# A 64 KB-strided transfer of sixteen half rows in front of all loads of a rotation kernel

## The chip, the cores and the metric

The kernel runs on one core of a Trainium2 chip. The metric is the device time of one execution in microseconds (us). A core has a matrix engine (TensorE, not used here), VectorE, ScalarE and GpSimd for computing, SyncE for issuing transfers, and 16 DMA engines that carry the transfers between the device memory (HBM) and the core's memory (SBUF, 128 partitions).

## The reference

A batch of 32 x 3 pictures of 256 x 256 float32 values is rotated by 90 degrees; nothing is calculated on the values.

```python
x = np.random.randn(32, 3, 256, 256).astype(np.float32)

def reference(x):
    return np.rot90(x, k=-1, axes=(-2, -1)).astype(np.float32)
```

That is 25.17 MB in and 25.17 MB out. Output row i of a picture is input column i read from the bottom up, so each picture is transposed and mirrored.

## The kernel before

**Tiling.** All 24,576 input rows (32 x 3 x 256, 1 KB each) are held in SBUF at once, in four groups of 2, 2, 4 and 4 units; a unit is 2048 rows, 16 KB in each of the 128 partitions. Each group has a tile of its own (`u0` to `u3`, printed as `u` in the profile), so no buffer is used for a second load. Three scratch tiles stand beside them: `spare` (two halves in PSUM), `extra` and `most`.

**Loads.** SyncE issues all of them, in the order in which they are written, on one hardware queue. Group 0 comes first and in two transfers: L67 brings the first 1024 rows (1 MB, eight consecutive rows or 8 KB to each partition, into the last quarter of the tile), L68 the other 3 MB. Partition p of the first transfer takes rows 8p to 8p + 7, so eight neighbouring partitions hold 64 KB of consecutive input. Group 1 follows in two transfers of 2 MB (L79), groups 2 and 3 in two of 4 MB each (L42, the helper `wide`). That makes eight loads. None of them waits for anything.

**Compute.** VectorE turns 32 x 32 blocks (`turn`, L92), ScalarE copies (`copy`, L95). The helper `keep` ties each instruction of an engine to the one before it, so both engines run in the order in which the calls are written. VectorE's first transpose needs both transfers of group 0.

**Stores.** Eight, again issued by SyncE in order, behind all loads: group 0 first (L200, made to wait for a mark in ScalarE's order, and one through `wide`), then two each for groups 1 to 3 (L42). Each waits for VectorE and ScalarE to be done with its half of a group.

**Semaphores.** The framework gives every transfer one of eight DMA semaphores in turn. With eight loads and eight stores each semaphore serves one load and one store. At the end SyncE (L236) waits until all of them have reached their counts.

The lines that the change touches are the two loads of group 0:

```python
    ld = rows_of(rows_in, 0).rearrange("(b p r) w -> p b (r w)", b=4, p=P)
    home = groups[0].rearrange("p s f -> p (s f)").rearrange("p (b f) -> p b f", b=4)
    nc.sync.dma_start(out=home[:, 3], in_=ld[:, 0])
    nc.sync.dma_start(out=home[:, :3], in_=ld[:, 1:])
```

Of the kernel before, what the change touches and what calls it, by code (L numbers as in the profile page):

```python
# [9 lines left out]
def kernel(  # L10
# [14 lines left out]
    nc = tc.nc  # L25
    fp32 = mybir.dt.float32

    B, C, H, W = x.shape
    P = nc.NUM_PARTITIONS
    R = 16  # L30
# [30 lines left out]
    def rows_of(rows, n):  # L61
        return rows[first[n] * P * R : (first[n] + sizes[n]) * P * R]


    ld = rows_of(rows_in, 0).rearrange("(b p r) w -> p b (r w)", b=4, p=P)
    home = groups[0].rearrange("p s f -> p (s f)").rearrange("p (b f) -> p b f", b=4)
    nc.sync.dma_start(out=home[:, 3], in_=ld[:, 0])  # L67
    nc.sync.dma_start(out=home[:, :3], in_=ld[:, 1:])  # L68
    for n in range(1, len(sizes)):
        I = sizes[n]  # L70
        ld = rows_of(rows_in, n).rearrange("(a i m r) w -> i m a (r w)", a=2, i=I, m=P // I)
        to = groups[n].rearrange("p s f -> p (s f)").rearrange("p (a f) -> p a f", a=2)
        if I == 4:
            ld = rows_of(rows_in, n).rearrange("(a i m r) w -> a m i (r w)", a=2, i=I, m=P // I)
# [166 lines left out]
```

## Time and profile before

| | |
|---|---|
| median of 3 runs | 122.49 us (122.31 to 122.51) |
| profiled execution | 122.36 us |
| its span, from the first to the last instruction | 120.6 us |
| moved over HBM | 50.33 MB, 417 GB/s over the span |
| DMA queue, share of 16 engines | 97.4% |
| VectorE busy | 83.3 us (69%), 25 instructions |
| ScalarE busy | 41.9 us (35%), 22 instructions |
| first load (L67), issue to landing | 4.8 us, 1 MB |
| VectorE's first transpose starts | 13.09 us |

Times inside the execution are counted from the start of the span. A row of the page such as `DMA` or `GB/s` has 40 numbers, one for each fortieth of the span (3.0 us); a digit is a share in tenths. Queue rows give packets, megabytes, and the time that the packets took as a share of 16 engines' span. A row of the waits says who waited for whom: microseconds in total, times, the longest. `SPq` is SyncE's instruction queue, and `L` with a number is a line of the kernel; L236 is the end of the program. A row of the chain or of the timeline begins with the start and the length in microseconds. Besides these views the trace holds a record of each DMA packet (start, length, size) and of each semaphore's updates, from which a few numbers below are taken.

### The profile page before, as it was taken

The page shows a single profiled execution, that of the slowest core. Times are in us where ns is not written, and L with a number is a line of the kernel's source. Part 1 is how long each engine was busy: PE and PEld are TensorE (multiplying, and loading weights), DVE is VectorE, ACT ScalarE, POOL GpSimd, SP SyncE. Part 2 cuts the span into 40 slices and gives each one's busy share as a digit, 9 for nine tenths or more (in the row PEclk, how much of TensorE's full clock was granted, in tenths as well). Part 3 has the DMA queues.
Part 4 walks back from the last instruction along what each step waited for, and adds up shares of the span by engine and source line. Part 5 has one row for each costly group of instructions (what it writes and reads, how often), then busy time and mean ns, then how long its engine had stood idle before and what let it go on. Part 6 is the DMA issues. An engine that isn't in the chain of part 4 may idle for free.

```text
span 120.6 us, 124 instructions
## 1 busy us (share of the span) xinstructions
DVE 83.3 (69%) x25; ACT 41.9 (35%) x22; POOL 0.2 (0%) x4
## 2 busy tenths in 40 slices
DVE  0000699999999999999999999999999900000000
ACT  0000400006910099937859389808302900000000
POOL 0000000000000000000000000000000000000000
DMA  3999999998989899999989999999898989898983
GB/s 95 429 427 427 454 429 435 435 500 370 489 380 489 380 435 435 413 457 402 467 370 500 391 478 391 478 391 478 380 489 380 489 380 489 370 500 359 511 359 163
DMA packets 2368, 50.33 MB, mean 417 GB/s; under 512 B 256, under 2 KB 256, under 8 KB 256
## 3 DMA queue, kind: packets, MB, share of 16 engines
q1 hardware_dynamic: 2368, 50.33, 97.4%
HBM read 25.17 MB, written 25.17 MB: 417 GB/s over the span
## 4 chain that ended last, share of the span: by engine, by line
DVE 68%; DMA 10%; issue 2%; SPq 0%; DVEq 0%
DVE u L92 48%; DVE spare L92 13%; DMA u<-in_x_dram 10%; DVE extra L92 5%; DVE most L92 2%; SPq L67 0%; DVEq L92 0%
## 5 line engine op out<-in xcount | busy, mean ns | idle before, releaser
L92 DVE STREAM_TRANSPOSE u<-u 128x2048 f32<-128x2048 f32 x15 | 56.0, 3792 | 0.2
L92 DVE STREAM_TRANSPOSE spare<-u 128x2048 f32<-128x2048 f32 (+1 forms) x4 | 11.7, 2946 | 13.1 <-DMA u<-in_x_dram 13.1
L95 ACT COPY u<-spare 128x2048 f32<-128x2048 f32 (+2 forms) x9 | 13.2, 1518 | 6.7 <-DVE spare L92 3.8
L95 ACT COPY spare<-u 128x2048 f32<-128x2048 f32 x2 | 7.6, 3811 | 8.9 <-DMA u<-in_x_dram 8.8
L95 ACT COPY extra<-u 128x1024 f32<-128x1024 f32 (+1 forms) x3 | 6.4, 2122 | 2.0 <-DMA u<-in_x_dram 2.0
L95 ACT COPY u<-extra 128x1024 f32<-128x1024 f32 (+2 forms) x4 | 6.0, 1670 | 2.7 <-DVE extra L92 2.7
L95 ACT COPY u<-u 128x2048 f32<-128x2048 f32 x1 | 1.9, 1899 | 13.7 <-DVE u L92 13.7
L95 ACT COPY u<-most 128x1792 f32<-128x1792 f32 x1 | 3.3, 3287 | 7.3 <-DVE u L92 7.3
L95 ACT ACT_TABLE_LOAD x1 | 1.3, 1283 | 13.1 <-DMA u<-in_x_dram 13.1
L92 DVE STREAM_TRANSPOSE spare<-spare 128x2048 f32<-128x2048 f32 x2 | 4.6, 2308 | 0.0
L92 DVE STREAM_TRANSPOSE u<-extra 128x2048 f32<-128x2048 f32 x1 | 4.0, 4004 | 0.0
L92 DVE STREAM_TRANSPOSE extra<-u 128x2048 f32<-128x2048 f32 x1 | 3.9, 3895 | 0.0
L95 ACT COPY most<-u 128x1792 f32<-128x1792 f32 x1 | 3.2, 3217 | 0.0
L92 DVE STREAM_TRANSPOSE extra<-extra 128x2048 f32<-128x2048 f32 x1 | 2.3, 2312 | 0.0
L92 DVE STREAM_TRANSPOSE most<-most 128x1792 f32<-128x1792 f32 x1 | 2.0, 1991 | 0.0
L225 POOL MEMSET const-bfloat16-1.0<- 128x1 bf16 x1 | 0.1, 102 | 0.0
L225 POOL MEMSET const-uint8-127<- 128x1 uint8 x1 | 0.1, 102 | 0.0
L225 POOL MEMSET const-float32-0.0<- 128x1 f32 x1 | 0.1, 100 | 0.2 <-issue 0.2
L225 POOL MEMSET const-float32-1.0<- 128x1 f32 x1 | 0.1, 99 | 0.0
## 6 DMA issues: line engine op xcount, KB each, us to landing
u<-in_x_dram SPq DMA_DIRECT2D x4, 4096.0 KB, 43.0
out_dram<-u SPq DMA_DIRECT2D x4, 4096.0 KB, 19.3
out_dram<-u SPq DMA_DIRECT2D x4, 2048.0 KB, 14.7
u<-in_x_dram SPq DMA_DIRECT2D x2, 2048.0 KB, 18.3
u<-in_x_dram SPq DMA_DIRECT2D x1, 3072.0 KB, 11.8
u<-in_x_dram SPq DMA_DIRECT2D x1, 1024.0 KB, 4.8
```

The source lines that it names most:

```text
L92: keep(nc.vector.transpose(out=out, in_=in_))
L95: keep(nc.scalar.copy(out=out, in_=in_))
L225: nc = _bacc.Bacc("TRN2", target_bir_lowering=False, num_devices=1)
```

## The change

A strip of 16 partitions with 128 float32 values each (512 bytes a partition) is allocated behind all other SBUF tiles. In front of the two loads of group 0, SyncE issues a transfer into it: of the partitions' rows in the first load's view every eighth (`ld[::P // R, 0]`, with P = 128 and R = 16), and of each the first 128 values. So it reads 16 pieces of 512 bytes whose starts are 64 KB apart; these are the first half of input rows 0, 64, 128 and so on up to 960. The first load reads the same bytes again into its own place. Nothing reads the strip.

```diff
     ld = rows_of(rows_in, 0).rearrange("(b p r) w -> p b (r w)", b=4, p=P)
     home = groups[0].rearrange("p s f -> p (s f)").rearrange("p (b f) -> p b f", b=4)
+
+    strip = ctx.enter_context(tc.tile_pool(name="strip", bufs=1)).tile([R, W // 2], fp32, name="strip")
+    nc.sync.dma_start(out=strip, in_=ld[::P // R, 0, : W // 2])
     nc.sync.dma_start(out=home[:, 3], in_=ld[:, 0])
     nc.sync.dma_start(out=home[:, :3], in_=ld[:, 1:])
     for n in range(1, len(sizes)):
```

## The prediction

> **What bounds the kernel now.** I read the page's DMA rows first, because the kernel moves 50.33 MB and computes nothing but transposes.
>
> ```profile
> DMA  3999999998989899999989999999898989898983
> GB/s 95 429 427 427 454 429 435 435 500 370 489 380 489 380 435 435 413 457 402 467 370 500 391 478 391 478 391 478 380 489 380 489 380 489 370 500 359 511 359 163
> q1 hardware_dynamic: 2368, 50.33, 97.4%
> ```
>
> The 16 DMA engines are busy from the second slice to the last but one: one queue, issued by SyncE alone, holds them 97.4% of the span. Only the first slice (3 tenths) and the last are open. So the end is fixed by the moment the engines begin to stream, plus 50.33 MB at their pace, as long as the queue never runs dry. The next views ask whether it does.
>
> ```profile
> SPq L42 <- DVE u L92: 27.8, 2, 20.2
> SPq L236 <- DMA out_dram<-u: 20.9, 3, 9.7
> 57.99 0.66 SPq L200 DMA_DIRECT2D out_dram<-u  x1
> 58.69 39.96 SPq L42 DMA_DIRECT2D out_dram<-u  x7
> ```
>
> The first two lines are SyncE's waits, the last two its issues in the timeline. SyncE issues the last store at 97.40, then waits 20.9 us at the end for DMAs (L236). By the semaphore records the last load lands at 61.63, when the first store (57.99) has been in the queue for 3 us. The last two stores, issued at 96.76 and 97.40, have 3 us in hand before the store ahead of them lands at 100.40. The queue never empties, so VectorE's chain, which the page shows as 68% of the span, is covered; it ends at 96.69.
>
> The change sits at the other end, so the chain of waits up to the first transpose comes next:
>
> ```profile
> 0.67 0.06 issue
> 0.73 0.40 SPq L67
> 1.12 0.06 issue
> 1.18 11.80 DMA u<-in_x_dram
> 12.98 0.03 issue
> ```
>
> And the same stretch in windows of 0.25 us. The columns at the end are the granted clock, the engines' busy share (a packet counted where it starts) and GB/s:
>
> ```profile
> 1.50:1.75 0.25, 0.00 (x0) 0.00 (x0) 0.00 (x0) 1.00 0.00 0
> 1.75:2.00 0.25, 0.00 (x0) 0.00 (x0) 0.00 (x0) 1.00 1.42 262
> 2.00:2.25 0.25, 0.00 (x0) 0.00 (x0) 0.00 (x0) 1.00 0.37 66
> 2.25:2.50 0.25, 0.00 (x0) 0.00 (x0) 0.00 (x0) 1.00 0.20 66
> 2.50:2.75 0.25, 0.00 (x0) 0.00 (x0) 0.00 (x0) 1.00 0.78 295
> 2.75:3.00 0.25, 0.00 (x0) 0.00 (x0) 0.00 (x0) 1.00 1.03 426
> ```
>
> Full pace is 426 GB/s, reached at 2.75. The packet records say how it gets there. A first batch of eight engines starts its first 8 KB packet at 1.77 to 1.96; the second batch of eight starts at 2.54 to 2.69, 0.77 us behind. In the first batch a first or second packet takes 0.46 to 1.06 us where the steady packet takes 0.309, and all of these long ones but one end between 2.78 and 2.90. Nothing like it occurs later. Each engine has a fixed share of the rows, so **the last engine to start sets the end**. It starts at 2.688, its second packet at 3.051; with the steady step of 0.306 per packet its virtual start is 3.051 - 0.306 = 2.745. The 16 landings of the first load are spread over 0.49 us, those of the last store over 0.54: the start's spread is carried through to the end.
>
> **The change part by part.**
>
> *One more issue on SyncE.* The strip's copy is issued first and L67 behind it. The nearest row is L67's own 0.397 us (128 rows, one dimension); L68 takes 0.419, and the loads of two dimensions 0.62 to 0.72. The strip has 16 rows in one dimension, so I take 0.397, with 0.72 as the upper end. The lower end is nothing: no row shows what an issue of 16 rows costs. With the gap of 0.058 to the next issue (1.125 to 1.183) the first load is issued 0.455 us later. Every later load moves by as much on SyncE's queue, and costs nothing there, because the transfers queue behind the first. L67's issue has no cover: SyncE's barrier ends at 0.67 and no other engine is moving data.
>
> *16 packets of 512 B and their 16 semaphore writes.* The load is landed by 16 engines; I take one row of the strip to each, at the address where that engine's share of the first load begins (its eight rows of 8 KB are 64 KB). Bounds: the 4-byte packet takes 0.009 us, the 8 KB packet 0.309. By size a row is 512/8192 x 0.309 = 0.02 us, with its semaphore 0.03 us. Engines that are idle until the load's descriptors come hide it; without that cover it is 0.03 us.
>
> *One more user of the eight DMA semaphores.* There are eight loads and eight stores for eight semaphores; with the strip the eighth load shares the strip's, and may wait for it before its issue. That issue comes at 5.11 + 0.455 = 5.57. The first load, 128 times as large, lands at 5.54, and the strip stands ahead of it, so I take nothing; if that issue did wait, it has until about 52 us, when its turn in the queue comes. The stores move by one semaphore together with the loads. At the end SyncE waits for the same eight.
>
> *What is behind it.* VectorE's first transpose waits for L67 and L68, so it shifts with the loads; so do all stores. The 3 us in hand at 61.63 and at 100.40 stay as they are, since both sides shift alike. Nothing else on VectorE, ScalarE or GpSimd is touched, and the strip's 512 bytes per partition are allocated behind all other tiles.
>
> *What the strip does to the start of the load behind it.* This is the one unknown. After the change the last engine may begin the load as late against its own issue as now: +0.455. Or the slow start belongs to the first use of the queue and is spent on the strip. If it were wholly gone and all engines started the load as far behind its issue as the very first does now (1.04 us), the last would start at 1.183 + 1.04 = 2.22, which is 2.22 - 2.745 = -0.52. So the ends are -0.52 and, with the dearest issue, 0.72 + 0.06 = +0.78. I take the first reading, +0.455. The eight late engines are late as a batch of half the 128 rows, and their packets are not stretched (0.31 to 0.38): they look as if they wait for the first batch's rows to be set up, as each new issue must have it done, rather than for a memory that is still asleep.
>
> The Trainium skill, page "DMA: Bandwidth & Descriptors", section "Latency and other measured facts", gives about 600 ns to the first byte of a DMA issued from SyncE. The trace agrees for the first batch, 1.77 - 1.125 = 0.64 us behind the end of the issue, and not for the second, 1.41 us. If that figure held for all engines once the queue is in use, an estimate from that page would have the load start by 1.58 + 0.6 = 2.18 and the run some 0.5 us faster, as the second rival below has it from rows alone; no transfer in this trace starts in an empty queue but the first, so the trace cannot decide.
>
> *Sum.* 122.36 (profiled execution: span 120.58 and 1.78 around it) + 0.455 = 122.81. The median of the runs, 122.49, is 0.13 above that execution, and so the forecast is 122.49 + 0.455 = **122.94**, slower by 0.37%.
>
> **The rivals.**
>
> *The slow start is paid once, at a fixed time (no change that can be told).* The strip's row waits where the load's first packet waits now. For it: the long packets end together at 2.78 to 2.90 although they started up to 0.58 us apart, as at one event. Then the late batch gets its strip row at 2.54 to 2.69 and the load 0.03 later: +0.03. Engines of the first batch that hold their strip until 2.89 start the load there with nothing read yet, at 2.89 against 2.745: +0.15. Result 122.52 to 122.64. Against it: four of the first eight packets took only 0.35 to 0.45, so there was no general standstill.
>
> *The strip wakes the path (faster).* The start-up is short for 16 packets of 512 B, and the load finds all engines ready: first start 2.22, the last one up to 0.19 later (the first batch's own spread), 2.41. Against 2.745 that is -0.52 to -0.33: 121.97 to 122.16, centre 122.1. It decides as soon as the last engine starts the load before 2.745 - 0.245 = 2.50. For it: the second batch waits about as long as eight rows on each of eight engines may take to set up (64 rows in 0.77 us, 12 ns each), and the strip has one row each, 0.1 us. Against it: by the same reckoning the load's own second batch would wait again, and nothing shows that a second set-up is quicker.
>
> On this rival the Trainium skill, same page, section "Two DMAs through the same engine are not ordered", says that descriptors of one queue start in order but are pipelined, so the load need not wait for the strip's write. No run here shows that yet; it would leave the forecast alone and take weight from the next rival.
>
> *The lag twice, or a dearer issue (slower by more).* The issue costs 0.62 to 0.72 as the two-dimensional loads do, or the load's set-up starts only when the strip is through at 2.89: +0.65 to +0.9, about 123.2.
>
> **How the numbers follow.** Differences under 0.2% (0.245 us) I count as no change: the three runs of before span 122.31 to 122.51. Forecast (+0.3 to +0.6): 0.49. Wake-up (faster): 0.25. Paid once (same): 0.20. Twice or dearer: 0.06. Slower is 0.49 + 0.06 = 0.55. The range starts at 122.05, inside the wake-up's 121.97 to 122.16 so that most of it is held, and ends at 123.10, the forecast's +0.6; that leaves out some 0.10 below and 0.07 above. The forecast's own range is 122.79 to 123.10. Cases of both signs hold most of the chance, so the range is one of 0.9% about a start-up of 1 us.
>
> **What would show it.** Right: in the changed profile SyncE's queue has one more issue of about 0.4 us ahead of the load's at about 1.18; the rise to 426 GB/s comes at about 3.2 instead of 2.75; the first load lands at about 6.0 instead of 5.54, the first transpose starts at about 13.54 instead of 13.09; and the end moves by as much. Full pace by 2.4 would show the wake-up, by 2.8 that the start-up is paid once. The prediction is wrong if the second batch is late only in the queue's first transfer. If the first transpose starts later and the end does not move, or the reverse, then the reading that the queue never runs dry was wrong.

## The result and the profile after

| | before | after |
|---|---|---|
| median | 122.40 us (6 runs, 122.31 to 122.51) | 122.92 us (6 runs, 122.87 to 122.99) |
| profiled execution's span | 120.6 us | 121.1 us |
| first load issued | 0.73 | 1.18 |
| first load landed (last engine) | 5.53 | 6.02 |
| first transpose starts | 13.09 | 13.58 |
| last load landed | 61.63 | 62.12 |
| last store landed | 119.76 | 120.23 |

The changed kernel takes 1.0042 times as long, with a 95% interval of 1.0029 to 1.0055. The forecast was 122.94, slower by 0.455 us; measured is 0.52 between the medians and 0.47 between the last landings of the two traces. That 122.94 and 122.92 lie so close is partly luck: the kernel before came out at 122.40 here, 0.09 under the 122.49 that the forecast starts from, and the change is 0.065 larger than its 0.455.

The chain of waits up to the first transpose, answering the one of before:

```profile
0.73 0.39 SPq L69
1.12 0.06 issue
1.18 0.41 SPq L70
1.58 0.04 issue
1.62 11.86 DMA u<-in_x_dram
13.48 0.03 issue
```

L69 is the strip's issue, L70 the first load's (L67 before), L71 the second's. Ahead of the DMA stand now two issues of about 0.4 us, and the DMA's own stretch is as long as it was: from L71's issue 11.86, before 11.80.

The windows at the start (granted clock, the engines' busy share, GB/s at the end of a row; a packet is counted where it starts):

```profile
1.75:2.00 0.25, 0.00 (x0) 0.00 (x0) 0.00 (x0) 1.00 0.13 31
2.00:2.25 0.25, 0.00 (x0) 0.00 (x0) 0.00 (x0) 1.00 0.56 131
2.25:2.50 0.25, 0.00 (x0) 0.00 (x0) 0.00 (x0) 1.00 0.72 131
2.50:2.75 0.25, 0.00 (x0) 0.00 (x0) 0.00 (x0) 1.00 0.89 131
2.75:3.00 0.25, 0.00 (x0) 0.00 (x0) 0.00 (x0) 1.00 0.59 164
3.00:3.25 0.25, 0.00 (x0) 0.00 (x0) 0.00 (x0) 1.00 0.52 164
3.25:3.50 0.25, 0.00 (x0) 0.00 (x0) 0.00 (x0) 1.00 0.87 360
3.50:3.75 0.25, 0.00 (x0) 0.00 (x0) 0.00 (x0) 1.00 1.08 459
```

The 31 GB/s from 1.75 to 2.00 are the strip. Its 16 packets take 0.025 us each, start on the 16 engines between 1.74 and 1.98 without any batch, and have landed by 2.29. Then the load's start comes as it was before, only later: eight engines at 2.22 to 2.30, the other eight at 2.96 to 3.03, first or second packets of up to 1.1 us, the long ones ending at 3.01 to 3.57, and full pace from about 3.3 to 3.5 instead of 2.75.

The waits of SyncE and the DMA queue, the rest of the span:

```profile
SPq L42 <- DVE u L95: 27.8, 2, 20.2
SPq L239 <- DMA out_dram<-u: 20.6, 1, 20.6
q1 hardware_dynamic: 2400, 50.34, 97.1%
```

Thirty-two more packets, 16 of 512 B and 16 semaphore writes, and otherwise the same: the queue never runs dry, and every time of the table after the first load's issue is 0.47 to 0.50 us later.

### The profile page after: what moved, and what is told of

Same layout as the page of the kernel before. It is cut to its first block, busy times and chain, and to the rows that moved or that the text cites. A ratio compares the mean times of both kernels' runs of the same rounds, so it can differ in the third digit from the quotient of the medians.

```text
span 121.1 us, 125 instructions
## 1 busy us (share of the span) xinstructions
DVE 83.5 (69%) x25; ACT 42.0 (35%) x22; POOL 0.2 (0%) x4
## 4 chain that ended last, share of the span: by engine, by line
DVE 67%; DMA 10%; issue 2%; SPq 1%; DVEq 0%
DVE u L95 48%; DVE spare L95 13%; DMA u<-in_x_dram 10%; DVE extra L95 5%; DVE most L95 2%; SPq L70 0%; SPq L69 0%; DVEq L95 0%
## 5 line engine op out<-in xcount | busy, mean ns | idle before, releaser
L95 DVE STREAM_TRANSPOSE u<-u 128x2048 f32<-128x2048 f32 x15 | 56.6, 3830 | 0.2
```

The lines of the kernel that those rows point to most:

```text
L95: keep(nc.vector.transpose(out=out, in_=in_))
```

## The experiments

Three explanations stood against each other at first. **A**: the cost is the strip's issue on SyncE in front of the first load; its packets are nearly free and the load's own start-up stays as it is. **B**: the 16 packets, or the early read, disturb the load. **C**: the strip takes over a part of the start-up, and the issue hides that gain. All ratios are to the kernel before, run on the same chip beside each kernel.

### The strip from another queue

```diff
-    nc.sync.dma_start(out=strip, in_=ld[::P // R, 0, : W // 2])
+    nc.scalar.dma_start(out=strip, in_=ld[::P // R, 0, : W // 2])
```

> The strip's copy is issued from ScalarE's queue; all loads are as in the kernel before. Theory A (the cost is the strip's issue standing in front of L67 on SyncE; its 16 packets are nearly free and the load's own start-up is not changed by them): the first load is issued at 0.73 again, its first batch of engines starts at about 1.77 and the second at about 2.5 to 2.7, and the median is that of before within 0.1 us (ratio 0.999 to 1.001). Rival B (the 16 packets on the engines, or the early read of the same rows, disturb the load): still about +0.3 to +0.5 us, ratio 1.003 to 1.004. Rival C (the strip takes over part of the start-up, hidden in the changed kernel by the issue): faster than before by 0.2 to 0.5 us, first load landing before 5.4.

Measured: 122.46 us, ratio 1.0004 (0.9995 to 1.0012). With the strip still there and only its issue moved to ScalarE, the cost is gone. From the timeline, and the windows of that kernel:

```profile
0.72 0.40 ACTq L69 DMA_DIRECT2D strip<-in_x_dram  x1
0.72 0.38 SPq L70 DMA_DIRECT2D u<-in_x_dram  x1
```

```profile
2.00:2.25 0.25, 0.00 (x0) 0.00 (x0) 0.00 (x0) 1.00 1.09 197
2.25:2.50 0.25, 0.00 (x0) 0.00 (x0) 0.00 (x0) 1.00 0.47 98
2.50:2.75 0.25, 0.00 (x0) 0.00 (x0) 0.00 (x0) 1.00 0.00 0
2.75:3.00 0.25, 0.00 (x0) 0.00 (x0) 0.00 (x0) 1.00 1.34 557
```

Both issues run side by side. The second batch of engines did start earlier, at 2.17 to 2.37, against the expectation; but its first packets took 0.6 to 0.73 us, no packet at all begins between 2.50 and 2.75, and all engines come free together at 2.84 to 2.98. The first load landed at 5.52, before at 5.53. B asked for +0.3 to +0.5 and C for -0.2 to -0.5, and neither is there. One thing this run can't show: the strip's own packets ran only from 2.84 to 2.98, behind the load's first ones, so it has no packets in front of the load. The strip of 128 rows below has eight times as many there.

### The strip behind the first load

```diff
-    nc.sync.dma_start(out=strip, in_=ld[::P // R, 0, : W // 2])
     nc.sync.dma_start(out=home[:, 3], in_=ld[:, 0])
+    nc.sync.dma_start(out=strip, in_=ld[::P // R, 0, : W // 2])
```

> The strip's copy stands behind L67 instead of in front of it. Theory A: L67's issue is back at 0.73 and the other issues come 0.45 us later, which costs nothing since the first load keeps every engine busy for about 2.5 us; what is left is 0.025 + 0.009 us of packets on each engine. Median +0.0 to +0.1 us against before. Rival B: the packets' own cost stays wherever they stand, +0.3 to +0.5 us.

Measured: 122.54 us, ratio 1.0009 (1.0000 to 1.0018), that is +0.11. The same issue and the same packets, one place later on the same queue, cost a fifth of what they cost in front. The expectation's upper end was +0.1; the packets account for 0.025 + 0.009 of it, another 0.04 or so lies between the last landing and the end of the span (see the shared semaphore below), and the remainder is at the edge of what these runs resolve.

### Two strips

```diff
-    strip = ctx.enter_context(tc.tile_pool(name="strip", bufs=1)).tile([R, W // 2], fp32, name="strip")
-    nc.sync.dma_start(out=strip, in_=ld[::P // R, 0, : W // 2])
+    strip = ctx.enter_context(tc.tile_pool(name="strip", bufs=1)).tile([2 * R, W // 2], fp32, name="strip")
+    for n in range(2):
+        half = slice(n * W // 2, (n + 1) * W // 2)
+        nc.sync.dma_start(out=strip[n * R : (n + 1) * R], in_=ld[::P // R, 0, half])
```

> Two strips in front, each of sixteen half rows (the second reads the other halves, into 16 more partitions). Theory A: the first load is issued 2 x 0.45 = 0.90 us later than before, its first packets start at about 2.67, and the median is +0.85 to +1.0 us against before, about 123.3. Rival B or C (the cost or the gain is that of the first use): the second strip adds less than 0.2 us, median +0.4 to +0.65.

Measured: 123.49 us, ratio 1.0090 (1.0076 to 1.0104), +1.06. The chain of this kernel (L71 the strips, L72 the first load):

```profile
0.73 0.39 SPq L71
1.11 0.06 issue
1.17 0.41 SPq L71
1.58 0.04 issue
1.62 0.42 SPq L72
2.04 0.04 issue
2.09 11.79 DMA u<-in_x_dram
```

The load is issued at 1.62, 0.89 us later than before; its two batches start at 2.69 and 3.44, again about 0.75 apart, though the queue has by then been used twice. The last landing is 1.01 later. The second strip costs as much as the first, so the slow start isn't one of first use. The median is 0.06 above the expected range, which had nothing for the end of the program: the span ends 0.91 us behind the last landing, in the kernel before 0.82.

### The strip from other rows

```diff
-    nc.sync.dma_start(out=strip, in_=ld[::P // R, 0, : W // 2])
+    far = rows_of(rows_in, 3)[: P * 8].rearrange("(p r) w -> p (r w)", p=P)
+    nc.sync.dma_start(out=strip, in_=far[::P // R, : W // 2])
```

> The changed kernel with the strip read elsewhere: sixteen half rows 64 KB apart from the beginning of the last group, which the first load doesn't touch. Theory A (only the place of the issue counts): as the changed kernel, +0.4 to +0.6 us against before, first load's issue at 1.18 and its landing at about 6.0. Rival B or C (the early read of the load's own addresses helps or harms it, beside the issue): the load's first packets differ from the changed kernel's and the median lies 0.1 us or more off 122.92.

Measured: 122.93 us, ratio 1.0044 (1.0031 to 1.0057); first load landed at 6.02, last store at 120.23, both as in the changed kernel. Which rows the strip reads makes no difference; that they are rows which the first load reads again neither helps nor harms.

### A strip of 128 rows

```diff
-    strip = ctx.enter_context(tc.tile_pool(name="strip", bufs=1)).tile([R, W // 2], fp32, name="strip")
-    nc.sync.dma_start(out=strip, in_=ld[::P // R, 0, : W // 2])
+    strip = ctx.enter_context(tc.tile_pool(name="strip", bufs=1)).tile([P, W // 2], fp32, name="strip")
+    nc.sync.dma_start(out=strip, in_=ld[:, 0, : W // 2])
```

> The strip takes a half row for each of the 128 partitions: 128 packets of 512 B, eight to an engine, 64 KB in all instead of 8 KB. It tells what the lag of the second batch of eight engines goes by. If by the number of rows that are set up: the strip's own packets come in two batches, the second some 0.7 us behind the first, and the load behind it is set up only after that, so the first load lands later than in the changed kernel by 0.3 to 0.7 us. If by bytes, or by the size of a packet: all 16 engines start the strip by about 2.0, the load starts in two batches at 2.2 and 2.96 as in the changed kernel, and the median is +0.45 to +0.7 (0.2 us of packets, mostly covered). The issue on SyncE stays at about 0.4 us.

Measured: 123.00 us, ratio 1.0052 (1.0038 to 1.0065), +0.57; first load landed at 6.11. The windows:

```profile
1.75:2.00 0.25, 0.00 (x0) 0.00 (x0) 0.00 (x0) 1.00 0.34 90
2.00:2.25 0.25, 0.00 (x0) 0.00 (x0) 0.00 (x0) 1.00 1.50 254
2.25:2.50 0.25, 0.00 (x0) 0.00 (x0) 0.00 (x0) 1.00 1.58 180
2.50:2.75 0.25, 0.00 (x0) 0.00 (x0) 0.00 (x0) 1.00 0.00 0
2.75:3.00 0.25, 0.00 (x0) 0.00 (x0) 0.00 (x0) 1.00 0.90 229
```

The strip's 128 packets all start between 1.76 and 2.33, without a gap of 0.7 us between two batches; the load behind has its second batch from 2.88 on, as in the changed kernel. Eight times the packets and bytes in front of the load add less than 0.1 us to the changed kernel, which leaves B little. So the number of rows alone isn't what the second batch waits for.

### Cutting the first load instead

If a small issue in front must be paid, it might at least bring data that is needed. The first load of the kernel before was cut at row k into runs of neighbouring partitions, for k = 16, 32 and 64:

```diff
-    nc.sync.dma_start(out=home[:, 3], in_=ld[:, 0])
+    nc.sync.dma_start(out=home[:k, 3], in_=ld[:k, 0])
+    nc.sync.dma_start(out=home[k:, 3], in_=ld[k:, 0])
```

> The kernel before with its first load cut in two: 16 rows of 8 KB (one packet to an engine), then the other 112. Like the strip it puts an issue of 16 rows in front, but one that brings data the kernel needs. Theory D (the slow start, eight engines 0.7 us behind and stretched packets, belongs to a transfer of large packets that meets idle engines): the 16 rows have it themselves, their packets end at about 2.8 to 2.9; the other 112 are issued at 1.18 and their start-up runs beside that; the engines stream from about 2.9 to 3.0 and the median is -0.1 to +0.25 us against before. Theory E (every transfer has its start-up, and short ones have none): the 16 packets run at once, 1.75 to 2.3, the last engine begins the 112 rows at about 2.96, and the median is -0.15 to +0.0. Both stand against +0.45, which is what the strip's issue in front costs when it brings nothing.

> As before, cut at 32 rows (two packets to an engine), then 96. Theory D: the first transfer has the slow start, and the second is set up meanwhile; streaming from about 2.9, -0.1 to +0.1 us. Theory E: engines start between 1.75 and 2.1, have work until 2.4 to 2.7, and the rest follows nearly without a gap: -0.3 to -0.5 us, 121.9 to 122.1.

> As before, cut in halves of 64 rows (four packets to an engine). Theory D: as the uncut load, 0.0 to +0.1 us, since the first transfer has the slow start and the second is hidden behind its 1.2 us of packets. Theory E, if the lag goes by the number of large packets: the second batch is half as late (0.35 us), -0.2 to -0.4 us.

Measured, against 122.40 beside them: 123.67 (ratio 1.0103, 1.0090 to 1.0116), 123.85 (1.0118, 1.0105 to 1.0131) and 124.71 (1.0187, 1.0174 to 1.0200). Neither D nor E had this in it. The start was as E has it in one respect: in the first two, all 16 engines began between 1.74 and 2.03, with no second batch. The time is lost after the start. Windows of the cut at 64:

```profile
3.00:4.00 1.00, 0.00 (x0) 0.00 (x0) 0.00 (x0) 1.00 1.24 295
4.00:5.00 1.00, 0.00 (x0) 0.00 (x0) 0.00 (x0) 1.00 0.83 180
5.00:6.00 1.00, 0.00 (x0) 0.00 (x0) 0.00 (x0) 1.00 1.01 221
6.00:7.00 1.00, 0.00 (x0) 0.00 (x0) 0.00 (x0) 1.00 1.15 238
```

The same windows of the kernel before:

```profile
3.00:4.00 1.00, 0.00 (x0) 0.00 (x0) 0.00 (x0) 1.00 0.97 410
4.00:5.00 1.00, 0.00 (x0) 0.00 (x0) 0.00 (x0) 1.00 0.99 418
5.00:6.00 1.00, 0.00 (x0) 0.00 (x0) 0.00 (x0) 1.00 1.12 467
6.00:7.00 1.00, 0.00 (x0) 0.00 (x0) 0.00 (x0) 1.00 0.97 410
```

The engines are busy (0.83 to 1.24) and move little more than half of what they moved before. Of the first 128 packets of 8 KB only 9 take less than 0.32 us (11 and 21 with k = 16 and 32), where before it is 109; their median is 0.61 us (0.49 and 0.50 with k = 16 and 32), before 0.31.

The next two kernels test whether that is the cut itself (G) or the partitions in which the engines meet (F): the same load cut by every fourth or every second partition. The thought was that each engine then keeps the partitions it has in the uncut load; the packet records name neither engine nor partition, so that isn't shown.

```diff
-    nc.sync.dma_start(out=home[:, 3], in_=ld[:, 0])
+    for m in range(k):
+        nc.sync.dma_start(out=home[m::k, 3], in_=ld[m::k, 0])
```

> [...] The cuts into runs of neighbouring partitions streamed at 180 to 295 GB/s instead of 410 during the first load. Theory F (that loss comes from the partitions which the engines meet in; a transfer of few rows starts all 16 engines within 0.3 us): no packet of about 0.5 us after the start, all engines start by about 2.05, two packets each by about 2.9, and the following transfers, 0.45 us apart in issue, join without a gap: 0.0 to -0.4 us against before, 122.0 to 122.4. Theory G (the loss comes from cutting the load, through more transfers and semaphores): packets of 0.45 to 0.55 us again, +0.8 to +1.6 us.

> The same cut into two, the even and the odd partitions, 64 rows each. Theory F: as e_mod4, but the first issue takes about 0.6 us, as it did for 64 neighbouring rows; first packets at about 2.0 to 2.4, streaming from about 2.9: -0.15 to +0.1 us. Theory G: as the cut into halves, +2 us.

Measured: cut in two (k = 2) 122.97 us, ratio 1.0060 (1.0037 to 1.0083); in four 125.21, 1.0240 (1.0222 to 1.0258). The first has the packets that F asks for, and its windows compare directly with those of the cut at 64:

```profile
3.00:4.00 1.00, 0.00 (x0) 0.00 (x0) 0.00 (x0) 1.00 1.00 385
4.00:5.00 1.00, 0.00 (x0) 0.00 (x0) 0.00 (x0) 1.00 0.96 393
5.00:6.00 1.00, 0.00 (x0) 0.00 (x0) 0.00 (x0) 1.00 0.98 385
6.00:7.00 1.00, 0.00 (x0) 0.00 (x0) 0.00 (x0) 1.00 1.06 426
```

Both have 64 rows to a transfer and two transfers; only which 64 differs, and 102 of the 128 packets are normal again. So the halved pace goes by which 64 rows stand in one transfer. That may be by the partitions they are written to or by the input rows that are read, which change together; no run here separates the two. The Trainium skill, page "SBUF — State Buffer", section "Door 1: The DMA port swizzle", says that partitions 0 to 63 reach only half of the 16 memory ports and so half of the bandwidth; the 180 to 295 GB/s against 385 to 426 here agree with it, for each half in turn. For the cuts at 16 and 32, whose second transfer reaches partitions of both halves, what stretches the packets was not tested.

But F's gain didn't come either. The issue of 64 rows takes 0.59 us instead of 0.40, so the first packets start at 2.11 instead of 1.77, and most first packets are stretched as before (0.5 to 1.3 us). In four it is far worse than F allows: the four issues take 0.57 to 0.59 each, by the packet records the engines' idle time grows by 8.5 us, summed over the 16 engines, between 3.0 and 9.0, where it doesn't grow in the kernel before, and the landings of one load spread over 1.5 us. Why 32 rows to every fourth partition run dry like that isn't settled by these runs.

Cut by columns, with each partition's first 2 KB ahead:

```diff
-    nc.sync.dma_start(out=home[:, 3], in_=ld[:, 0])
+    nc.sync.dma_start(out=home[:, 3, : 2 * W], in_=ld[:, 0, : 2 * W])
+    nc.sync.dma_start(out=home[:, 3, 2 * W :], in_=ld[:, 0, 2 * W :])
```

> The kernel before with its first load cut by columns: of each of the 128 partitions first 2 KB (eight packets of 2 KB to an engine, 0.08 us each by size), then the other 6 KB. The strip of 128 rows showed that 128 packets of 512 B start on all 16 engines between 1.76 and 2.02 without a lag. If the lag goes by the size of the packets, the 2 KB packets start nearly as those, all engines have work from about 1.8 to 2.6, and the second transfer's start (first batch 2.22, second 2.96) is half covered: -0.2 to -0.4 us against before. If it goes by the bytes asked for at once, the slow start appears with the 2 KB packets or comes back whole with the 6 KB ones: -0.05 to +0.3 us.

Measured: 123.15 us, ratio 1.0063 (1.0050 to 1.0077), +0.75: outside both ranges. The 2 KB packets do come in two batches: eight engines start at 1.73 to 2.0, and no more than eight are at work until others join at 2.45 to 2.55. So the second batch is seen with 128 rows of 8 KB and of 2 KB, at much the same distance (0.7 to 0.8 us), and not with 128 rows of 512 B or with 16, 32 or 64 neighbouring rows of 8 KB (64 start between 2.12 and 2.44): it takes many rows and packets that are not small. What it waits for stays open.

### Two queues for group 0

```diff
-    nc.sync.dma_start(out=home[:, :3], in_=ld[:, 1:])
+    nc.scalar.dma_start(out=home[:, :3], in_=ld[:, 1:])
```

> The kernel before with the second transfer of group 0 (L68, 3 MB) issued from ScalarE at the same time as L67 from SyncE. With the strip on ScalarE's queue the second batch of engines began the first load at 2.17 to 2.37 instead of 2.54 to 2.69, but all engines came free together at 2.84 to 2.98. If the second queue shortens the start-up when it brings needed data too: all engines are at work by about 2.4, -0.1 to -0.3 us against before. If the engines come free only at about 2.9 whatever is asked for: -0.05 to +0.1 us.

Measured: 130.66 us, ratio 1.0677 (1.0662 to 1.0691). At the start it went as the second reading has it (full pace at 2.75 as before), and what follows was foreseen by neither. Rows of the DMA queues and of the page:

```profile
DMA  3999999899899899897005989999799799799793
q1 hardware_dynamic: 1968, 47.19, 85.7%
q10 hardware_dynamic: 400, 3.15, 5.8%
```

The two queues share the engines, so L68's 3 MB on `q10` now run beside the loads of the groups behind and land at 23.09 instead of 12.98. VectorE starts its first transpose at 23.12, the first store, which waits for ScalarE's mark, goes 10 us later (67.73 instead of 57.99), and the loads are through at 61.76: the hole of about 8 us in the DMA row (the digits 0, 0 and 5) is the loss of 8.3. It is the case in which the queue does run dry, and it shows what the 3 us in hand of the kernel before are worth.

No kernel tried here was faster than the kernel before.

## Why the prediction was right

**The bound.** Confirmed. A delay of the first load reached the last store almost unchanged, 0.48 and 0.47 us. With two strips the first load landed 0.91 later and the last store 1.01; the 0.1 between them appears in one place, between the landings of the seventh load (+0.90) and the eighth (+1.01), and isn't explained. The 3 us in hand did not quite stay as they were: the first store was issued 0.76 later and the last one 0.66, against 0.47 to 0.50 for the loads. Enough was left for it to cost nothing.

**One more issue on SyncE, 0.455 us.** Right in size and as the mechanism. The strip's issue took 0.389, the load was issued 0.447 later. The row taken, L67's 128 rows, fits an issue of 16 rows; 0.72 as the upper end wasn't needed. Its reason was misread, too: L68 has two dimensions like the loads at 0.62 to 0.72, and takes 0.42. That it is the place of the issue, and not what it moves, is shown by the strip from ScalarE (+0.03), behind the first load (+0.11), from other rows (+0.52) and twice (+1.06).

**The packets.** 0.025 us for 512 B, estimated 0.02 by size. They were over by 2.01, before the load's first packet at 2.22, and so were hidden as said. That each engine got the row with which its share of the load begins was assumed and isn't shown, since the records name no engine; the strip from other rows says that nothing hangs on it.

**The shared semaphore.** SyncE's issue of the eighth load did wait on the strip's semaphore, at 5.53, where 5.57 had been worked out; the strip had landed at 2.29, and the issue began without delay. The end of the program, which "waits for the same eight" and was put at nothing, did cost a little: from the last landing to the end of the span it is 0.82 us in the kernel before, 0.85 to 0.86 in every kernel here with one more transfer, 0.91 with two more and 0.98 with three more. The semaphore of the last store no longer stands last in SyncE's row of waits (it is the strip's), so one wait more comes behind it. With this 0.034 the terms give the span's growth: 0.447 for the issue, 0.037 at the load's start, 0.034 at the end, less 0.013 on the way, together 0.505 us.

**The last engine's start.** The sum had it move by the issue alone, 2.745 to 3.200. The engine that was last by its second packet began that one at 3.530, a virtual start of 3.224: +0.479. The second batch began a little sooner against its issue (3.03 - 1.175 = 1.86 us, before 1.96), but first packets in it took up to 0.555 us instead of 0.384. The two nearly cancel, which the sum did not foresee and which is luck. Full pace came at 3.3 to 3.5, not at the 3.2 named as a sign.

**The reason given for the forecast's reading was wrong in one half.** That each transfer of this shape has its slow start, whatever went ahead, is shown (after one strip, after two, after 128 rows). That the second batch waits "for the first batch's rows to be set up" does not hold by rows alone: 128 rows of 512 B had no second batch. Nor does it go by bytes, since rows of 2 KB wait as long as rows of 8 KB. The choice between the readings came out right on a reason that was only half right.

**The rivals.** Paid once: falls with the two strips. The wake-up: the short start-up of 16 small packets was there, as it assumed (1.74 to 1.98), and the second half of it, that the load then finds all engines ready, was not (2.96 to 3.03). Its rule from the Trainium skill, page "DMA: Bandwidth & Descriptors", section "Latency and other measured facts", about 600 ns to the first byte, agrees with the strip (0.63 us behind the end of its issue for the first of the engines) and with the load's first batch (2.22 - 1.58 = 0.64), and again not with its second batch (1.37), now on a queue already in use. The lag twice: the load did not wait for the strip's lag, since the strip had none; the load's first packet began at 2.22, before the strip's last landing at 2.29.

## What to carry to other kernels

Where one queue is full from start to end, whatever stands in front of its first transfer is added to the whole run: here 0.45 us an issue, however little it moves, while the same issue one place further back, or on an idle engine's queue, costs next to nothing (0.11 and 0.03). Before a warm-up is bought, look whether the slow start belongs to the queue's first use or to each transfer of that shape; put two warm-ups in front and see whether the second one is free. And a transfer moved to a second queue shares the engines with everything behind it, so it can land far later than in its turn.

## What the runs showed of the hardware that was not expected

- A load of 128 rows to an idle set of engines starts on eight of them first and on the other eight 0.66 to 0.8 us later, with packets of 8 KB and of 2 KB, but not with packets of 512 B, nor with 16, 32 or 64 neighbouring rows of 8 KB. With the strip issued from ScalarE at the same time it was 0.42.
- Cutting a 1 MB load at partition 64 nearly halved its pace (180 to 295 GB/s against 410 to 467); cutting it into even and odd partitions did not (385 to 426).
- An issue of 64 rows, to neighbouring or to every second partition, took 0.57 to 0.61 us on SyncE, as did 32 rows to every fourth; 16, 32, 96, 112 and 128 rows to neighbouring partitions took 0.38 to 0.42. Behind the dear issues that of the 3 MB load was dear as well, 0.59 instead of 0.42 to 0.43, so the number of rows isn't all of it.
- Each transfer more left 0.03 to 0.07 us more between the last landing and the end of the span.
- On two queues, 3 MB beside the other queue's loads took until 23.09 us to land, instead of 12.98 in their turn on one queue.
